# Products of zeros in the scan's chain of a hybrid encoder layer

## The chip, the cores and the metric

One core of one Trainium2 chip runs the program. The metric is the device time of one execution in microseconds; the profile that is quoted comes from one further execution, taken by the hardware profiler. TensorE is called PE (its weight loads PEld), VectorE DVE, ScalarE ACT, GpSimd POOL and SyncE SP. SP issues most DMAs, POOL and ACT some.

## What is computed

One encoder layer over 1024 tokens of width 1024: a SwiGLU feed-forward network, a mixing layer, and a second feed-forward network, each normalised before and after and added to its input. The mixing layer has eight attention heads and eight heads of a recurrence (RWKV-7) that runs forward and backward over the sequence. The change lies in the recurrence:

```python
def _rwkv7_step(state, inp):
    r, w, k, v, kk, kka = inp
    sa = jnp.einsum('dbhvk,dbhk->dbhv', state, kk)
    state = state * w[..., None, :] - sa[..., :, None] * kka[..., None, :] + v[..., :, None] * k[..., None, :]
    y = jnp.einsum('dbhvk,dbhk->dbhv', state, r)
    return state, y
...
    _, ys = lax.scan(_rwkv7_step, state0, xs)
```

## The kernel before

The program runs through in one line: the first feed-forward network (products `gu` on L81, `pd` on L415), the projections of the mixing layer, attention, the scan, the output projection, and the second feed-forward network. The scan is the part between about 1300 and 1595 us of the profile.

The recurrence is computed in chunks of 64 tokens, two chunks to a block, 16 chunks in 8 blocks, both directions and all heads at once. Per block there are four steps. `prep` loads the decays, keys and receptances of the block, forms the scaled operands `pt` and `bk` on DVE and ACT, and multiplies them on PE into the chunk matrices `lp`, which DVE masks into `lm` (L832, three PSUM buffers); `bp` are transposes of `bk`, which ACT copies to `bt`. `solve` inverts triangular pieces of 32x32 on DVE, in 31 steps of a product (`ttmp`, L866) and a difference (`Ti`, L868), each step waiting for the one before. `merge` joins two pieces on PE (`pa`, L894, and `pb`, L900, of 32x32) into `tt`. `chain` carries the state from chunk to chunk. `prep` and `solve` of later blocks run ahead of the chain (three blocks at the most), and between the blocks the attention's part of the output projection is done (`yq`, `po`, 512 columns each): its products fill PE where the chain waits.

For each chunk `chain` does the following. The products `xu` of the chunk's matrix with the state `sv` (L941) are copied to `xs` by ACT (L944); `xs` is multiplied by `tt` into the same bank (L952), and ACT writes the result with its sign turned into `uv`, in two halves (L954). The bank `st` gathers the old state (by an identity, L949) and the products of `uv` with `bt` (L960); DVE scales it into the next chunk's `sv`, again in two halves (L968). The bank `y` gathers the products of the state with the receptances (L958, `y<-pr,sv`) and those of `uv` with `lm` (L963, `y<-lm,uv`); ACT copies it to `yb` (L970), which a DMA stores after the block. The products that are added to a bank go through one helper, so that the profile has them all on L937. In the first chunk of all the state is zero and the products with it are left out. `xu`, `st` and `y` have one PSUM bank each, which holds 512 values per partition. Each product of this chain is of 64 columns in 32-bit floats, which PE runs as two instructions, so the profile counts two where the program has one; the products `po` are of a rounded 32-bit type and are one instruction each.

A scheduler decides the order in which each engine gets its instructions, from the program's order, the dependencies and its own estimates of durations. Within an engine the instructions then run in that order. The scan's tiles lie in one pool, `sc`: first the two `tt` tiles (made in `scan_inverses`), then an unused tile `edge` of 112 values per partition, then the tiles of the chain. The function that ties the steps together is `run`; it calls `scan_inverses` on L1276 and opens the pools around it.

Of the kernel before, what the change touches and what calls it, by code (L numbers as in the profile page):

```python
# [10 lines left out]
F32 = mybir.dt.float32  # L11
F32R = mybir.dt.float32r
AF = mybir.ActivationFunctionType
# [150 lines left out]
class _Kernel:  # L164
# [753 lines left out]
    def chain(self, n, blk, c, psum):  # L918


        nc, V, A, T = self.nc, self.nc.vector, self.nc.scalar, self.nc.tensor
        heads = [(d, pr, par) for d in range(2) for pr in range(4) for par in range(2)]
        half = lambda par: slice(par * 64, par * 64 + 64)
        ls, lm, tt, gc, bt, pt = slice(n * TB, (n + 1) * TB), blk["lm"], blk["tt"], blk["gc"], blk["bt"], blk["pr"]
        YB = [c.tile([128, 4, TB], F32, name="yb", tag=f"yb{d}") for d in range(2)]
        for d in range(2):
            for par in range(2):
                A.copy(lm[half(par), par, d, :, :, 0:64],
                       pt[d][half(par), :, :, 0:C].rearrange("p a i t -> p i a t"))
        for i in range(BLK):  # L930
            ch = n * BLK + i
            first = ch == 0
            uv = c.tile([128, 2, 2, 4, 64], F32, name="uv", tag="uv", bufs=2)
            self.values(uv, ch)
            sv, nx = self.states(ch, c), self.states(ch + 1, c)
            bank = lambda nm: psum.tile([128, 2, 4, 64], F32, name=nm, tag=nm, bufs=1)
            add = lambda o, a, b, start, stop: T.matmul(o, a, b, start=start, stop=stop, skip_group_check=True)  # L937
            xu, st, y = bank("xu"), bank("st"), bank("y")
            for d, pr, par in heads:
                ks = half(1 - par) if first else slice(0, 128)  # L940
                T.matmul(xu[half(par), d, pr, :], lm[ks, par, d, i, pr, 0:64], sv[ks, d, par, pr, :], start=True,  # L941
                         stop=True)
            xs = c.tile([128, 2, 4, 64], F32, name="xs", tag="xs")
            A.copy(xs, xu)  # L944
            if not first:
                for d in range(2):
                    for par in range(2):
                        hs = half(par)
                        add(st[hs, d], self.ident[hs, hs], sv[hs, d, par], d == 0, False)  # L949
            for d, pr, par in heads:  # L950
                hs = half(par)
                T.matmul(xu[hs, d, pr, :], tt[hs, (d * BLK + i) * 4 + pr, :], xs[hs, d, pr, :], start=True, stop=True)  # L952
            for par in range(2):
                A.activation(uv[half(par), :, par], xu[half(par)], AF.Copy, scale=-1.0)  # L954
            if not first:
                for d, pr, par in heads:
                    hs = half(par)
                    add(y[hs, d, pr, :], sv[hs, d, par, pr, :], pt[d][hs, pr, i, 64:128], d == 0 and pr == 0, False)  # L958
            for d, pr, par in heads:
                add(st[half(par), d, pr, :], bt[d][:, i, par, pr, :], uv[:, d, par, pr, :],  # L960
                    first and d == 0 and pr == 0, True)
            for d, pr, par in heads:
                add(y[half(par), d, pr, :], uv[:, d, par, pr, :], lm[:, par, d, i, pr, 64:128],  # L963
                    first and d == 0 and pr == 0, True)
            if nx is not None:
                for par in range(2):
                    hs = half(par)
                    V.tensor_tensor(nx[hs, :, par], st[hs], gc[hs, :, :, i:i + 1].to_broadcast([64, 2, 4, 64]), op=OP.mult)  # L968
            for d in range(2):
                A.copy(YB[d][:, :, i * C:(i + 1) * C], y[:, d])  # L970
        for d in range(2):
            self.nc.scalar.dma_start(self.y_d[d][:, :, ls].rearrange("a p t -> p a t"), YB[d])
# [190 lines left out]
    def run(self):  # L1163
        nc = self.nc
# [4 lines left out]
        with self.top as top:  # L1169
# [8 lines left out]
            with ExitStack() as st:  # L1178
# [18 lines left out]
                for t in natural:  # L1197
                    a, b = xr[t % 4], xr[t % 4 + 4]
# [19 lines left out]
                p = self.pool(st, "ffn1")  # L1218
# [22 lines left out]
                y = [self.finish_low(rows, psum, ct, [ps[ct, half] for half in range(2)]) for ct in LO]  # L1241
# [31 lines left out]
            s_xn.close()  # L1273
            B0 = self.pool(s_sc, "blks", 1)
            sc = self.pool(s_sc, "scan")
            self.scan_inverses(sc)  # L1276
            sc.tile([128, 112], F32, name="edge")
            s_eo, s_pe = ExitStack(), ExitStack()
            eo = self.pool(s_eo, "eo")
            pc = self.pool(s_ps, "ps_c", 1, space=PSUM)  # L1280
# [92 lines left out]
            with ExitStack() as st:  # L1373
# [12 lines left out]
                p, hand = self.pool(st, "ffn2"), self.pool(st, "hand3")  # L1386
# [49 lines left out]
```

## Time and profile before

| | us |
|---|---|
| median of 3 runs | 2369.25 (2357.99 to 2371.84) |
| the profiled execution | 2369.46 |
| its span, first to last instruction | 2367.7 |
| PE busy in the span | 2212.2 |
| DVE busy | 1782.8 |
| ACT busy | 1034.4 |
| POOL busy | 608.7 |

A group of instructions in the profile is written as line, engine, operation, output and inputs, the operands' sizes and the count, then its busy time in us and the mean of one in ns, then the idle time of the engine just ahead and who ended it. For a product of PE the form 64*128 64x128 says that the weights fill 64 rows and 128 columns and that 128 columns of the other operand move through. PE's matmuls overlap each other, so that the spacing of their starts, not their length, tells what one costs. The granted clock is 1.00 where PE ran at its full clock.

### The profile page before, as it was taken

How to read it: one execution, taken by the hardware profiler on the slowest of the kernel's cores; microseconds unless marked ns; L12 is line 12 of the kernel's file. 1: busy time of each engine (PE TensorE's matmuls, PEld its weight loads, DVE VectorE, ACT ScalarE, POOL GpSimd, SP SyncE). 2: the span in 40 equal slices, each digit the busy share in tenths (PEclk: the TensorE clock that was granted, in tenths of full speed). 3: DMA queues.
4: the chain of work that ended last, by engine and by line, in shares of the span. 5: the costliest groups of instructions: out<-in, count | busy, mean ns of one | idle time of the engine just before them, and what ended most of it. 6: DMA issues, size and time to landing. Idle time of an engine off the chain costs nothing. (4 is left out here: it accounts for less than half of the span.)

```text
span 2367.7 us, 39507 instructions
## 1 busy us (share of the span) xinstructions
PE 2212.2 (93%) x14532; PEld 1784.9 (75%) x14532; DVE 1782.8 (75%) x2957; ACT 1034.4 (44%) x1958; POOL 608.7 (26%) x732
## 2 busy tenths in 40 slices
PE   6999999999999998999995889988799999999997
PEld 4788888878877676788774767765678888887886
DVE  8899999865676344667568767837889999987565
ACT  4322333354676413666545545445442333235453
POOL 6244443400000010111102242432334344441000
PEclk8999999999999998999996798989989999999999
DMA  5354445486652514322369676577534544447655
GB/s 156 107 174 151 170 146 170 167 266 193 220 185 98 193 42 134 91 81 71 94 161 223 165 183 176 151 208 256 178 95 168 174 167 154 169 153 265 195 188 181
DMA packets 359381, 386.04 MB, mean 163 GB/s; under 512 B 74258, under 2 KB 265618, under 8 KB 359188
## 3 DMA queue, kind: packets, MB, share of 16 engines
q1 hardware_dynamic: 308512, 276.43, 38.8%
q0 software_dynamic: 30320, 94.44, 11.3%
q10 hardware_dynamic: 20356, 12.66, 1.9%
q8 instruction: 114, 1.87, 0.3%
q14 instruction: 79, 0.65, 0.1%
HBM read 257.53 MB, written 125.89 MB: 162 GB/s over the span
## 5 line engine op out<-in xcount | busy, mean ns | idle before, releaser
L186 ACT ACTIVATE wh<-raw 128x512 fp32r<-128x512 f32 (+1 forms) x273 | 167.8, 626 | 264.1 <-DVE raw L62 95.0
L187 DVE TENSOR_TENSOR wl<-raw,wh 128x512 fp32r<-128x512 f32 (+1 forms) x273 | 277.6, 1020 | 3.1 <-ACT wh L186 2.0
L81 PE MATMUL gu<-xh,wh 128*128 128x512 f32 x704 | 277.9, 395 | 0.9 <-ACT xh L186 0.8
L81 PE MATMUL gu<-xl,wh 128*128 128x512 f32 x704 | 276.3, 393 | 0.0
L81 PE MATMUL gu<-xh,wl 128*128 128x512 f32 x704 | 276.2, 392 | 0.0
L415 PE MATMUL pd<-gl,gwh 128*128 128x512 f32 x616 | 240.4, 390 | 3.1 <-DVE gl L187 3.1
L415 PE MATMUL pd<-gh,gwh 128*128 128x512 f32 x616 | 239.6, 390 | 0.5 <-DVE row L86 0.5
L415 PE MATMUL pd<-gh,gwl 128*128 128x512 f32 x616 | 239.7, 389 | 0.0
L86 DVE TENSOR_TENSOR row<-gu,row 128x512 f32<-128x512 f32 x308 | 206.4, 682 | 23.2 <-PE gu L81 22.4
L187 DVE TENSOR_TENSOR gwl<-graw,gwh 128x512 fp32r<-128x512 f32 (+1 forms) x176 | 117.0, 667 | 129.7 <-ACT gwh L186 127.5
L116 POOL DMA_DIRECT2D d_hid<-row x154 | 84.7, 551 | 470.6 <-DVE row L114 444.2
L186 ACT ACTIVATE gwh<-graw 128x512 fp32r<-128x512 f32 (+1 forms) x176 | 101.4, 576 | 190.5 <-PE pd L415 162.2
L81 PEld LDWEIGHTS gu<-xh,wh 128*128 128x128 f32 x704 | 133.9, 190 | 29.5 <-ACT xh L186 2.0
L81 PEld LDWEIGHTS gu<-xl,wh 128*128 128x128 f32 x704 | 133.8, 190 | 27.9
L81 PEld LDWEIGHTS gu<-xh,wl 128*128 128x128 f32 x704 | 133.3, 189 | 27.5
L415 PEld LDWEIGHTS pd<-gl,gwh 128*128 128x128 f32 x616 | 115.6, 188 | 28.5 <-DVE gl L187 4.9
L415 PEld LDWEIGHTS pd<-gh,gwh 128*128 128x128 f32 x616 | 115.5, 188 | 25.6 <-DVE row L86 0.8
L415 PEld LDWEIGHTS pd<-gh,gwl 128*128 128x128 f32 x616 | 115.6, 188 | 23.8
L94 ACT ACTIVATE row<-row 128x512 f32<-128x512 f32 x44 | 27.9, 633 | 223.9 <-DVE row L86 216.4
L187 DVE TENSOR_TENSOR gl<-raw,gh 128x512 fp32r<-128x512 f32 x160 | 112.9, 717 | 15.7 <-ACT gh L186 15.4
L145 POOL TENSOR_TENSOR ws<-ws 128x512 f32<-128x512 f32 x88 | 114.4, 1300 | 1.2
L186 ACT ACTIVATE gh<-raw 128x512 fp32r<-128x512 f32 x160 | 98.0, 621 | 32.2 <-DMA raw<-in_ffn_w_down_dram 21.1
(356 smaller groups left out, 5353.4 us busy)
## 6 DMA issues: line engine op xcount, KB each, us to landing
d_hid<-row POOLq DMA_DIRECT2D x154, 256.0 KB, 2.5
graw<-d_hid SPq DMA_DIRECT2D x132, 256.0 KB, 3.0
raw<-in_ffn_w_gate_dram SPq DMA_DIRECT2D x88, 256.0 KB, 3.1
raw<-in_ffn_w_up_dram SPq DMA_DIRECT2D x88, 256.0 KB, 3.3
ws<-in_ffn_w_down_dram SPq DMA_DIRECT2D x88, 256.0 KB, 4.5
d_ws<-ws POOLq DMA_DIRECT2D x88, 256.0 KB, 2.3
raw<-d_ws SPq DMA_DIRECT2D x88, 256.0 KB, 2.7
raw<-in_ffn_w_down_dram SPq DMA_DIRECT2D x66, 256.0 KB, 3.3
```

The source lines that it names most:

```text
L81: self.K.nc.tensor.matmul(ps, a[:, k, :], b[:, k, :], start=(k == 0 and i == 0), stop=(k == 3 and i == 2))
L86: add = lambda o, x: V.tensor_tensor(o, ps, x, op=OP.add)
L94: A.activation(y[:, 0], y[:, 0], AF.Silu)
L116: put = lambda n, y: G.dma_start(self.hid[n - 1, j // 2], y)
L145: G.tensor_tensor(o, a, b, op=OP.subtract)
L186: self.nc.scalar.activation(h, src, AF.Copy)
L187: (eng or self.nc.vector).tensor_tensor(l, src, h, op=OP.subtract)
L415: T.matmul(ps[x], a[:, ts], b, start=(m == 0 and k == 0), stop=(m == NM - 1 and k == 2))
```

## The change

A tile `zero` of 128x512 is written once, as a copy of the identity scaled by 0.0, ahead of the scan. A helper adds two products of it with itself (128x128 of it as weights, 512 columns) to a bank, with neither the start nor the stop flag. It is called on the bank `y` at two places of each chunk: after the products of `y` with the state (not in the first chunk of all, which has none) and after the products of `y` with `uv`. The tile `edge` is opened ahead of `zero` and of the `tt` tiles instead of after them.

```diff
@@ chain
             bank = lambda nm: psum.tile([128, 2, 4, 64], F32, name=nm, tag=nm, bufs=1)
             add = lambda o, a, b, start, stop: T.matmul(o, a, b, start=start, stop=stop, skip_group_check=True)
+
+            def add_nothing(o):
+
+                for _ in range(2):
+                    add(o.rearrange("p a b c -> p (a b c)"), self.zero[:, :128], self.zero, False, False)
+
...
                     add(y[hs, d, pr, :], sv[hs, d, par, pr, :], pt[d][hs, pr, i, 64:128], d == 0 and pr == 0, False)
+            if not first:
+                add_nothing(y)
             for d, pr, par in heads:
                 add(st[half(par), d, pr, :], bt[d][:, i, par, pr, :], uv[:, d, par, pr, :],
...
                 add(y[half(par), d, pr, :], uv[:, d, par, pr, :], lm[:, par, d, i, pr, 64:128],
                     first and d == 0 and pr == 0, True)
+            add_nothing(y)
@@ run
             sc = self.pool(s_sc, "scan")
+            sc.tile([128, 112], F32, name="edge")
+            self.zero = sc.tile([128, 512], F32R, name="zero")
+            nc.scalar.activation(self.zero.rearrange("p (a b) -> p a b", a=4),
+                                 self.ident[:, None, :].to_broadcast([128, 4, 128]), AF.Copy, scale=0.0)
             self.scan_inverses(sc)
-            sc.tile([128, 112], F32, name="edge")
```

The scheduler draws a new order. On PE, the second chunk of the first block stood as follows before, from its first products to the `prep` of a later block (`lp`):

```order
L941 MATMUL xu<-sv,lm 64x64 x16
L937 MATMUL st<-sv,ident 64x256 x4
L952 MATMUL xu<-xs,tt_12089 64x64 x16
L937 MATMUL y<-pr,sv 64x64 x16
L937 MATMUL st<-uv,bt 64x64 x16
L937 MATMUL y<-lm,uv 64x64 x16
L830 MATMUL lp<-pr,bk 128x128 x16
```

The chain's products follow each other, with nothing of another step between them. The same chunk now, on PE, from the pair that ends the chunk before it:

```order
L937 MATMUL y<-zero 128x512 x2
L947 MATMUL xu<-sv,lm 64x64 x16
L937 MATMUL st<-sv,ident 64x256 x4
L958 MATMUL xu<-xs,tt_12092 64x64 x16
L937 MATMUL y<-pr,sv 64x64 x16
L937 MATMUL y<-zero 128x512 x2
L937 MATMUL st<-uv,bt 64x64 x16
L937 MATMUL y<-lm,uv 64x64 x16
L937 MATMUL y<-zero 128x512 x2
L830 MATMUL lp<-pr,bk 128x128 x16
```

Two pairs are new, one ahead of `st<-uv` and one ahead of `lp`; the rest keeps its order. On PE again, the beginning of the second block before, where `merge` (`pa`, `pb`) runs among the products that the chain can already do:

```order
L894 MATMUL pa<-d_12947,lm 32x32
L937 MATMUL st<-sv,ident 64x256 x4
L937 MATMUL y<-pr,sv 64x64 x7
L894 MATMUL pa<-d_12947,lm 32x32 x31
L937 MATMUL y<-pr,sv 64x64 x6
L941 MATMUL xu<-sv,lm 64x64
L937 MATMUL y<-pr,sv 64x64 x3
L1064 MATMUL po<-woh,yah 128x512
L1064 MATMUL po<-wol,yah 128x512
L1064 MATMUL po<-woh,yal 128x512
L900 MATMUL pb<-tt_12090,d_12947 32x32 x27
L830 MATMUL lp<-pr,bk 128x128 x16
```

The first `lp` of the next `prep` come after most of `pb`. The same place on PE now, from the rest of `pa`:

```order
L894 MATMUL pa<-d_12955,lm 32x32 x31
L937 MATMUL st<-sv,ident 64x256
L937 MATMUL y<-pr,sv 64x64 x5
L947 MATMUL xu<-sv,lm 64x64
L937 MATMUL y<-pr,sv 64x64 x11
L937 MATMUL y<-zero 128x512
L900 MATMUL pb<-tt_12093,d_12955 32x32
L937 MATMUL y<-zero 128x512
L900 MATMUL pb<-tt_12093,d_12955 32x32 x4
L1073 MATMUL po<-woh,yah 128x512
L900 MATMUL pb<-tt_12093,d_12955 32x32 x16
L1073 MATMUL po<-wol,yah 128x512
```

The two zero products stand one by one between the end of `y<-pr,sv` and `pb`, and the `po` among `pb` instead of ahead of it.

## The prediction

> **What bounds the kernel now.** I read the page first: the span, and the row of the granted clock, whose 40 slices are 59 us each.
>
> ```profile
> span 2367.7 us, 39507 instructions
> PEclk8999999999999998999996798989989999999999
> ```
>
> The clock's two lowest digits, 6 and 7, lie in the slices from 1243 to 1361 us, where the scan begins. So I cut the scan into its blocks, each from the first xu product of one block to that of the next, and asked for the busy times (PE, PEld, DVE, ACT, POOL, each with its count), the granted clock, and the DMA's share and GB/s.
>
> ```profile
> 1310.00:1353.80 43.80, 38.45 (x553) 30.86 (x551) 31.64 (x86) 22.78 (x43) 12.61 (x21) 0.73 0.69 181
> 1353.80:1400.00 46.20, 41.21 (x604) 33.24 (x604) 35.23 (x108) 21.44 (x41) 12.63 (x21) 0.93 0.64 173
> 1400.00:1443.50 43.50, 36.65 (x584) 30.01 (x582) 25.28 (x68) 20.30 (x40) 12.60 (x21) 0.80 0.74 167
> 1443.50:1480.00 36.50, 32.64 (x554) 26.64 (x552) 31.17 (x92) 18.36 (x36) 12.57 (x21) 1.00 0.77 196
> 1480.00:1517.20 37.20, 34.27 (x618) 29.54 (x618) 32.95 (x102) 21.38 (x41) 12.80 (x21) 0.86 0.58 143
> ```
>
> PE is busy for 84 to 92% of every block, more than DVE in each, and the one block with the full clock throughout takes 36.5 us against 43.5 to 46.2 for the first three. The waits of PE over these blocks come next (waiting line <- releaser: total us, times, longest).
>
> ```profile
> PE lp L830 <- DVE lm L832: 11.9, 6, 5.5
> PE st L937 <- ACT uv L954: 3.1, 6, 1.3
> PE xu L941 <- DVE sv L968: 1.0, 3, 0.4
> ```
>
> Those are the waits that border on the chain, about 16 us in the 250 us from 1310 to 1560. So inside the scan PE and its clock set most of the pace, and DVE follows closely. That the scan's length counts for the end is shown by the queue of SP: it held the loads of the stage behind the scan until a product of y freed their memory.
>
> ```profile
> SPq L182 <- PE y L937: 35.3, 1, 35.3
> ```
>
> **Where the clock falls.** The stretches at half clock between 1310 and 1560, same columns:
>
> ```profile
> 1326.50:1333.20 6.70, 6.70 (x51) 5.00 (x49) 3.19 (x10) 1.84 (x4) 2.90 (x5) 0.50 0.83 223
> 1337.00:1353.70 16.70, 15.61 (x127) 12.16 (x127) 13.54 (x37) 10.41 (x20) 0.00 (x0) 0.50 0.55 142
> 1381.10:1387.80 6.70, 6.70 (x32) 5.45 (x33) 6.31 (x18) 1.17 (x2) 0.00 (x0) 0.50 0.40 128
> 1418.60:1435.60 17.00, 13.61 (x108) 10.17 (x109) 13.01 (x40) 8.28 (x15) 0.00 (x0) 0.50 0.45 125
> 1480.10:1490.20 10.10, 8.73 (x174) 8.18 (x175) 7.88 (x28) 7.50 (x14) 1.19 (x2) 0.50 0.64 144
> ```
>
> PE was busy for 51.4 of these 57.2 us. At full clock that work would take about half, so the five falls cost PE up to 25.7 us. The starts are not far from whole multiples of 3.41 us apart, so I asked what PE did in the 3.41 us before a fall (matmuls only, weights and moving operand by form). The rows are 1333.26 to 1336.67 (three), 1377.63 to 1381.04 (one) and 1476.62 to 1480.03 (four), each just ahead of a fall, and 1459.55 to 1462.96 (two), after which the clock held.
>
> ```profile
> L937 PE MATMUL y<-pr,sv 64*64 64x64 f32 x20 | 1.4, 235 | 0.0
> L894 PE MATMUL pa<-d,lm 32*32 32x32 f32 x62 | 1.2, 192 | 0.0
> L941 PE MATMUL xu<-sv,lm 128*64 128x64 f32 x2 | 0.3, 246 | 0.0
> ...
> L830 PE MATMUL lp<-pr,bk 64*128 64x128 f32 x25 | 2.6, 291 | 1.5 <-DVE lm L832 1.5
> ...
> L894 PE MATMUL pa<-d,lm 32*32 32x32 f32 x62 | 1.4, 192 | 0.0
> L838 PE MATMUL bp<-ident,bk 64*128 64x64 f32 x9 | 0.9, 228 | 0.0
> L1075 PE MATMUL yq<-ident,yat 128*128 128x128 f32 x4 | 0.7, 286 | 0.0
> L941 PE MATMUL xu<-sv,lm 128*64 128x64 f32 x2 | 0.3, 246 | 0.0
> ...
> L830 PE MATMUL lp<-pr,bk 64*128 64x128 f32 x28 | 2.7, 279 | 1.2 <-DVE lm L832 1.2
> L838 PE MATMUL bp<-ident,bk 64*128 64x64 f32 x3 | 0.4, 238 | 0.0
> ```
>
> Count the moving columns, each weighted by the share of the 128 rows that it fills. Ahead of the falls that gives 20x64/2 + 62x32/4 + 2x64 = 1264, then 25x128/2 = 1600, then 496 + 288 + 512 + 128 = 1424; where the clock held, 28x64 + 3x32 = 1888. So in these four windows the clock falls when the weighted columns stay below some 1600 to 1900. That is an estimate from four windows, and two of them hold no long idle time at all. [...]
>
> **The change, part by part.** The new tile costs one ACTIVATE of 128x512 ahead of the scan, with nothing queued behind it that is due, and the renumbered memory moves no work: zero for both, and half a microsecond if ACT were the bound there. Each of the 31 places (16 after the last products of y, 15 after the products of y with the state) gets two products of 512 columns. The nearest row is po, the same operands in size and type; the timeline shows a single one and a pair between small products (start, length, form, count):
>
> ```profile
> 1449.50 1.10 PE L937 MATMUL y<-lm,uv 128*64 128x64 f32 x29
> 1450.54 0.50 PE L1064 MATMUL po<-woh,yah 128*128 128x512 f32 x1
> 1450.97 0.33 PE L941 MATMUL xu<-sv,lm 128*64 128x64 f32 x2
> 1451.22 0.50 PE L1064 MATMUL po<-wol,yah 128*128 128x512 f32 x1
> 1451.56 0.40 PE L1064 MATMUL po<-woh,yal 128*128 128x512 f32 x1
> 1451.89 0.33 PE L937 MATMUL y<-pr,sv 64*64 64x64 f32 x2
> ```
>
> The pair occupies 1451.22 to 1451.89 = 0.67 us, and the change of form ahead of it some 0.1 more: 0.78 us. 31 x 0.78 = 24 us of PE time at full clock.
>
> What lies under a wait: in the second chunk of a block the products of st wait for the second half of uv,
>
> ```profile
> 1319.59 1.53 PE L937 MATMUL st<-uv,bt 128*64 128x64 f32 x31
> 1366.40 1.09 PE L937 MATMUL st<-uv,bt 128*64 128x64 f32 x29
> ```
>
> 1.53 against 1.09 us where uv was there, so 0.44 us are free in each of 8 chunks, 3.5 us. Behind a block's end PE waits for DVE (the 11.9 us above); I take five of the six as block ends with room for 0.78 us, 3.9 us. Behind a block's first chunk it waits up to 0.4 us for sv, some 2 us in five blocks. Hidden: 9.4 us; left on PE: about 15 us. The bounds are 0 (DVE hides all of it) and 24 us (nothing is hidden). Queued behind a pair are the copies of y to yb, whose readers are DMAs, and the next xu or lp; 0.78 us later hurts through PE's order alone.
>
> What the pairs give: a pair adds 2x512 = 1024 weighted columns. In the window of 1333.26 the early products of y with the state would carry a pair: 1264 + 1024 = 2288, kept. In that of 1476.62 likewise, 1424 + 1024 = 2448, kept. In that of 1377.63 the block's last pair would reach in with about one product: 1600 + 512 = 2112, kept. Ahead of 1326.43 the pair comes a little too early, and the fall at 1418.6 follows the longest wait for DVE (5.5 us above), so both stay. Saved: half of 15.61 + 8.73 + 6.70 = 15.5 us of PE time; bounds 0 and 25.7.
>
> Sum: +15 - 15.5, about nothing on PE. The pairs' cost is surer than their effect on the clock (zeros might not count as work, and the windows' phase differs from run to run), so I take 13 of the 15.5: **+2 us**. The profiled execution took 2369.46 us (its span and 1.8 us around it), 0.2 us above the median of three runs, so the forecast is **2371 us**. The schedule is also drawn anew (front part: pa, pb and lp change places); nothing in the trace prices that, and I allow 8 us either way, a sixth of a block.
>
> **Rivals.** (1) Slower: the zeros don't hold the clock. Then the cost stands alone, and at half clock it is larger: 57.2 of 250 us are cold, and a product there takes about twice as long. 24 x (0.77 + 0.23 x 2) = 29.5 us without cover, 20 with the 9.4 us hidden: 2390 to 2399, say 2395. It decides if the falls come as often as before and the waits ahead of st<-uv go on beside the pairs. For it: the falls at 1326 and 1418 come from DVE's evictions, which no pair shortens. As a mechanism: if a fall needs a long idle time of PE, like the 5.5 us ahead of 1418.6, the pairs prevent none, since they only fill waits below 0.8 us. [...] Against it: four of the five falls had no wait as long. (2) Faster: the clock holds through the whole scan. 25.7 us saved less 0 to 15: 2344 to 2359; with the new schedule's 8 us on its side, down to 2336. For it: the 24 us by which the first three blocks exceed 36.5. Against it: DVE waited for DMAs there too. (3) DVE is the bound everywhere and neither part shows: 2369, within my forecast's own range. A form of the change that does nothing can't be: PE has the 62 products in its queue.
>
> **How the numbers follow.** Chances: the forecast's case with (3), 0.46, own range 2356 to 2384; the first rival 0.32; the second 0.22. A measurement of this kernel can tell about 1% (24 us) from no change. The first rival's 20 to 29.5 us straddle that, with the new schedule behind it; I count its chance as slower by over 1%, and that of the second, whose price reaches the 1% with full cover, as faster; what either loses to the middle I take as made up by the forecast's own tails under the new schedule. The range reaches to the price without cover, with a little of the schedule's 8 us above it, 2401, and down to the clock held under full cover, 2345.
>
> **What would show it.** Right: the zero pairs occupy 0.7 to 0.8 us and stand where st<-uv waited; the scan keeps one or two falls of the clock behind evictions, none among pa and pb; blocks stay between 36 and 46 us. Wrong, slower: as many cold stretches as before and blocks a pair or two longer each. Wrong, faster: the clock at 1.00 from 1310 to 1560 and every block near 36.5 us. The stages outside the scan should stand as they are.

## The result, and the profile after

The changed kernel took 2382.9 us (median of 11 runs, 2371.5 to 2387.1) against 2370.7 us for the kernel before in the same session (11 runs): a ratio of 1.0051, 95% interval 1.0031 to 1.0070. It is slower by about 12 us. The profiled execution took 2382.9 us, 13.4 us more than the profiled execution before. The page's row of the granted clock in 40 slices of its span of 2381.1 us, after:

```profile
PEclk8999999999999998999996778998989999999999
```

The low digits, 6 and 7, stand where they stood, and a second 7 follows them, where a 9 was. The scan cut at the ends of its blocks (a block ends where its yb goes to memory), the same five blocks before and, in the second fence, after; the columns are those of the prediction (the window and its length, busy time and count of PE, PEld, DVE, ACT and POOL, the clock, the DMA's share and GB/s).

```profile
1324.40:1377.90 53.50, 46.02 (x597) 36.38 (x599) 39.49 (x119) 24.41 (x46) 16.44 (x28) 0.78 0.64 165
1377.90:1415.20 37.30, 34.22 (x592) 28.47 (x591) 24.20 (x64) 20.66 (x40) 12.46 (x21) 0.91 0.72 174
1415.20:1460.00 44.80, 38.44 (x602) 31.28 (x601) 33.28 (x99) 20.91 (x40) 7.54 (x12) 0.81 0.67 163
1460.00:1498.30 38.30, 33.39 (x580) 28.39 (x578) 32.60 (x100) 20.21 (x39) 12.72 (x22) 0.87 0.69 172
1498.30:1531.40 33.10, 31.91 (x588) 26.80 (x587) 26.05 (x78) 17.40 (x33) 13.07 (x23) 1.00 0.55 147
```

```profile
1321.70:1373.30 51.60, 49.98 (x618) 38.61 (x616) 37.57 (x114) 23.64 (x45) 10.83 (x19) 0.74 0.65 166
1373.30:1427.60 54.30, 46.60 (x611) 35.72 (x611) 32.10 (x92) 21.29 (x41) 16.80 (x29) 0.78 0.61 152
1427.60:1465.70 38.10, 35.74 (x591) 28.80 (x589) 25.80 (x70) 20.81 (x40) 8.06 (x15) 0.87 0.67 164
1465.70:1508.30 42.60, 37.51 (x607) 30.55 (x605) 35.74 (x111) 20.75 (x40) 14.35 (x24) 0.88 0.62 163
1508.30:1545.20 36.90, 35.46 (x592) 29.22 (x589) 26.04 (x78) 17.36 (x33) 15.09 (x24) 0.91 0.57 149
```

The five blocks take 223.5 us instead of 207.0. PE is busy for 205.3 us instead of 184.0, and its clock is no higher: 0.74 to 0.91 against 0.78 to 1.00. The largest step is the third block of the scan, the second row, 54.3 us instead of 37.3. There the order of DVE has changed, which the timelines of DVE (two rows) and PE (the third) show:

```profile
1415.11 0.69 DVE L1081 TENSOR_TENSOR yat<-yat,rs 128x512 f32<-128x512 f32 x1 [8.14 <-DMA yat<-d_ya]
1415.71 1.40 DVE L977 TENSOR_TENSOR sv<-st,gc 64x512 f32<-64x512 f32 x2
1416.45 0.48 PE L947 MATMUL xu<-sv,lm 128*64 128x64 f32 x2 [4.98 <-DVE sv L977]
```

A multiplication of `yat` stands ahead of the hand-over of the state `sv` and waits 8.14 us for its load; PE waits 4.98 us for `sv` behind it. It is the obvious suspect, and the experiments test it.

The half-clock stretches that began between 1310 and 1560 us, after, same columns:

```profile
1325.90:1353.10 27.20, 26.98 (x257) 20.16 (x257) 18.93 (x52) 14.74 (x27) 0.59 (x1) 0.50 0.58 152
1377.10:1394.10 17.00, 17.00 (x175) 12.31 (x174) 10.51 (x29) 8.97 (x16) 1.19 (x2) 0.50 0.53 154
1414.60:1421.40 6.80, 4.95 (x41) 3.59 (x43) 4.89 (x16) 0.58 (x1) 5.24 (x10) 0.50 0.50 107
1431.70:1441.90 10.20, 10.20 (x89) 7.17 (x88) 8.43 (x23) 4.51 (x9) 0.00 (x0) 0.50 0.18 59
1469.30:1479.40 10.10, 8.12 (x35) 6.58 (x36) 9.27 (x29) 5.33 (x11) 1.59 (x3) 0.50 0.54 164
1527.30:1534.00 6.70, 6.70 (x92) 5.52 (x85) 3.03 (x13) 2.27 (x4) 3.52 (x6) 0.50 0.41 81
```

Six falls instead of five, and 78.0 us at half clock instead of 57.2. To see where the zeros stood, I asked for their busy time alone (PE, PEld, ACT; then clock, DMA share, GB/s) in the 3.4 us ahead of each of the six falls:

```profile
1322.40:1325.80 3.40, 0.00 (x0) 0.00 (x0) 0.00 (x0) 1.00 1.18 251
1373.60:1377.00 3.40, 0.00 (x0) 0.00 (x0) 0.00 (x0) 1.00 1.11 284
1411.20:1414.60 3.40, 0.26 (x2) 0.00 (x0) 0.00 (x0) 1.00 1.03 257
1428.20:1431.60 3.40, 0.00 (x0) 0.00 (x0) 0.00 (x0) 1.00 1.13 274
1465.80:1469.20 3.40, 0.00 (x0) 0.00 (x0) 0.00 (x0) 1.00 0.76 187
1523.80:1527.20 3.40, 0.00 (x0) 0.00 (x0) 0.00 (x0) 1.00 0.16 23
```

Five of the six windows hold no product of zeros; in the sixth the end of a pair is all that PE did. PE's timeline at the end of the first block shows why:

```profile
1316.79 1.10 PE L937 MATMUL y<-pr,sv 64*64 64x64 f32 x32
1317.82 0.73 PE L937 MATMUL y<-zero 128*128 128x512 f32 x2
1318.48 1.15 PE L937 MATMUL st<-uv,bt 128*64 128x64 f32 x32
1319.46 1.10 PE L937 MATMUL y<-lm,uv 128*64 128x64 f32 x32
1320.49 0.73 PE L937 MATMUL y<-zero 128*128 128x512 f32 x2
1321.16 1.82 PE L830 MATMUL lp<-pr,bk 64*128 64x128 f32 x22
1324.03 0.93 PE L830 MATMUL lp<-pr,bk 64*128 64x128 f32 x8 [1.04 <-DVE lm L832]
```

Here the pairs lie among the chain's dense products. The poor stretch begins only behind the last pair, with the `lp` that wait for DVE, and the window that decides, from 1322.4, begins there too.

### The profile page after: what moved, and what is told of

It reads as the page before. It is cut to its first block, busy times and chain, and to the rows that moved or that the text cites. A ratio compares the mean times of both kernels' runs of the same rounds, so it can differ in the third digit from the quotient of the medians.

```text
span 2381.1 us, 39636 instructions
## 1 busy us (share of the span) xinstructions
PE 2243.0 (94%) x14594; PEld 1802.3 (76%) x14594; DVE 1783.2 (75%) x2957; ACT 1035.0 (43%) x1959; POOL 608.7 (26%) x732
```

## The experiments

One profile of one execution isn't enough here: the 11 runs of the changed kernel spread over 16 us. So beside the median I use the span and the mean granted clock that each run has. (1 - clock) x span is called the time lost to the clock, the rest the time beside it. This is bookkeeping, not a cause: half clock while PE waits is counted as lost too. Means with their standard errors, in us. The experiments ran in three sessions, (a), (b) and (c), on two chips, each with runs of the kernel before, which differ by 2 to 3 us in both columns. So ratios and differences are to the kernel before of the same session. For the session of the changed kernel the kernel before has no clock on record; it is compared with all three.

| kernel | zeros | median | ratio, 95% interval | lost to the clock | beside it |
|---|---|---|---|---|---|
| before (a) | none | 2368.1 | | 95.1 ± 1.5 | 2271.8 ± 0.8 |
| before (b) | none | 2369.1 | | 97.6 ± 1.3 | 2269.6 ± 0.8 |
| before (c) | none | 2367.4 | | 94.2 ± 1.5 | 2271.5 ± 1.0 |
| none (a) | none | 2374.5 | 1.0018 (1.0003 to 1.0034) | 101.0 ± 1.4 | 2270.2 ± 1.2 |
| n16 (b) | 31 pairs of 16 | 2368.7 | 1.0000 (0.9982 to 1.0019) | 95.3 ± 2.1 | 2271.2 ± 0.7 |
| end (b) | 16 pairs of 512 | 2369.8 | 1.0011 (0.9994 to 1.0028) | 98.5 ± 1.4 | 2270.4 ± 1.0 |
| mid (c) | 15 pairs of 512 | 2379.0 | 1.0045 (1.0027 to 1.0062) | 98.6 ± 1.4 | 2277.9 ± 1.1 |
| one (c) | 31 x 1 of 512 | 2374.8 | 1.0026 (1.0010 to 1.0042) | 98.5 ± 1.8 | 2274.0 ± 1.1 |
| n128 (a) | 31 pairs of 128 | 2380.7 | 1.0051 (1.0032 to 1.0071) | 101.5 ± 1.9 | 2277.0 ± 1.7 |
| pin4_n128 (c) | 31 pairs of 128 | 2383.4 | 1.0056 (1.0034 to 1.0077) | 102.4 ± 2.9 | 2278.0 ± 1.1 |
| after | 31 pairs of 512 | 2382.9 | 1.0051 (1.0031 to 1.0070) | 99.3 ± 1.9 | 2280.4 ± 1.7 |
| real (a) | 31 pairs of 512 | 2382.6 | 1.0058 (1.0038 to 1.0078) | 98.8 ± 3.6 | 2281.2 ± 1.7 |
| pin4 (a) | 31 pairs of 512 | 2385.4 | 1.0078 (1.0058 to 1.0099) | 108.1 ± 3.7 | 2276.7 ± 2.2 |
| four (b) | 31 x 4 of 512 | 2405.6 | 1.0155 (1.0127 to 1.0183) | 111.7 ± 2.5 | 2291.1 ± 1.1 |
| gap4 (b) | 4 a block, elsewhere | 2371.2 | 1.0013 (0.9992 to 1.0033) | 93.3 ± 2.0 | 2277.2 ± 0.8 |
| gap8 (c) | 8 a block, elsewhere | 2381.5 | 1.0072 (1.0045 to 1.0098) | 96.5 ± 2.5 | 2286.5 ± 1.5 |

So the 12 us of the change are, by the session that they are compared with, 8.6 to 10.8 us beside the clock (± 1.9) and 1.7 to 5.1 us lost to it (± 2.4). No kernel clearly beat the one before.

The two theories at the start: the price theory (TensorE's time for the zeros is what the change costs) and the order theory (the newly drawn order costs, the wait behind `yat` above all).

**No products.** Both calls of `add_nothing` on `y` are taken out; the tile and the moved edge stay.

```diff
-            if not first:
-                add_nothing(y)
...
-            add_nothing(y)
```

> The tile of zeros and the moved clearing edge stay, no product of zeros is issued; the order is drawn anew. Price theory: 2368 to 2373 us, as the kernel before. Order theory: a time that differs from the kernel before by some us either way, with the difference in single blocks where the order differs.

Measured: 2374.5 us, a ratio of 1.0018. The interval barely leaves out 1, and the 4 us are all in the clock's column: 5.9 ± 2.1 us more are lost to it, and beside it the kernel stands 1.6 ± 1.4 us below the one before. Setting up the tile and drawing the order anew cost nothing beside the clock; what the change costs there comes with the products. A few microseconds lost to the clock, on the other hand, need no product.

**Narrow products at the same order.**

```diff
-                    add(o.rearrange("p a b c -> p (a b c)"), self.zero[:, :128], self.zero, False, False)
+                    add(o.rearrange("p a b c -> p (a b c)")[:, :128], self.zero[:, :128], self.zero[:, :128], False, False)
```

> The pairs stay at their places but each product of zeros has 128 columns instead of 512, so the order on VectorE and ScalarE is that of the changed kernel. A pair should fall from 0.67 us to about 0.2 us, 31 x 0.47 = 14.5 us of TensorE time less. Price theory (the zeros' own TensorE time is what the change costs): the time falls by most of that, to 2369 to 2373 us, at or below the kernel before. Order theory (the rows' new order costs, above all the multiplication of yat ahead of sv in the third block): the third block stays near 54 us and the time near 2380 us. If the 512 columns did hold the clock up in part, the clock from 1310 to 1600 us falls below 0.85.

Measured: 2380.7 us, and in its profile a third block of 54.7 us, as the order theory had it. But the expectation mis-sized the pair. PE's timeline of this kernel at the same place:

```profile
1324.67 1.10 PE L937 MATMUL y<-pr,sv 64*64 64x64 f32 x32
1325.70 0.44 PE L937 MATMUL y<-zero 128*128 128x128 f32 x2
1326.07 1.16 PE L937 MATMUL st<-uv,bt 128*64 128x64 f32 x31
...
1328.16 0.44 PE L937 MATMUL y<-zero 128*128 128x128 f32 x2
```

From the pair's start to the next product it is 0.37 us (1325.70 to 1326.07), not 0.2; so 31 x 0.30 = 9.3 us of TensorE's time went, not 14.5. Of that 4.3 ± 2.4 us show beside the clock, against the kernel `real` below, which has pairs of 512 columns in the same session. Next came still narrower pairs, to see which theory the remaining 5.2 ± 1.9 us belong to.

```diff
-                    add(o.rearrange("p a b c -> p (a b c)"), self.zero[:, :128], self.zero, False, False)
+                    add(o.rearrange("p a b c -> p (a b c)")[:, :16], self.zero[:, :128], self.zero[:, :16], False, False)
```

> Pairs of 16 columns: next to no TensorE time, an order close to that of the changed kernel (in the third and fourth block a multiplication of yat still goes ahead of sv). Price theory: as the kernel without products, 2371 to 2376 us. Order theory: 2378 to 2383 us, as with 128 and 512 columns.

Measured: 2368.7 us, the time of the kernel before. A `yat` ahead of `sv` is in this order too: DVE waited 4.5 us for its load in the third block, though PE waited only 1.1 us for `sv` behind it. So the order theory's 2378 to 2383 us was missed by far, and the price theory's 2371 to 2376 us was 2 us too high.

**The wait for `yat`.** In the changed kernel, and in the kernel with 128 columns, the multiplication of `yat` for the fifth row tile is queued behind the third block's hand-over of `sv`.

```diff
-                    V.tensor_tensor(nx[hs, :, par], st[hs], gc[hs, :, :, i:i + 1].to_broadcast([64, 2, 4, 64]), op=OP.mult)
+                    done = V.tensor_tensor(nx[hs, :, par], st[hs], gc[hs, :, :, i:i + 1].to_broadcast([64, 2, 4, 64]), op=OP.mult)
+                if i == 0:
+                    self.handed[n] = done
...
+        with self.tc.issue_after(self.handed[t - 2].ins) if t in (4,) else ExitStack():
```

> The changed kernel with the multiplication of yat for the fifth row tile held behind the hand-over of sv in the third block, where the kernel before has it. Order theory: the wait of TensorE for sv there (5.0 us) and the clock fall behind it go, the third block falls from 54 us to 40 to 46 us, and the time to 2371 to 2376 us. Price theory: the third block shortens but the time stays at 2380 to 2384 us.

> Pairs of 128 columns, with the multiplication of yat for the fifth row tile held behind sv in the third block. Theory that the pairs of 128 columns cost 12 us only by the wait for yat (8.8 us of VectorE, 5 to 6 us of TensorE): 2368 to 2374 us, with 2270 to 2273 us beside the time lost to the clock (2277.0 with the wait). Theory that the products cost whatever their columns: 2377 to 2384 us, with 2275 us or more.

Measured: 2385.4 and 2383.4 us, neither faster than without the pin. The swap itself worked, as DVE's timeline of the pinned kernel with 512 columns shows, and its third and fourth blocks in windows:

```profile
1412.44 1.41 DVE L977 TENSOR_TENSOR sv<-st,gc 64x512 f32<-64x512 f32 x2 [2.94 <-PE st L937]
1417.30 0.69 DVE L1084 TENSOR_TENSOR yat<-yat,rs 128x512 f32<-128x512 f32 x1 [3.45 <-DMA yat<-d_ya]
```

```profile
1375.70:1421.70 46.00, 42.86 (x602) 33.10 (x598) 26.24 (x72) 21.28 (x42) 14.53 (x24) 0.81 0.69 162
1421.70:1464.90 43.20, 38.72 (x602) 31.87 (x604) 31.88 (x90) 20.88 (x41) 9.09 (x17) 0.84 0.65 162
```

`sv` goes first, the third block falls from 54.3 to 46.0 us, and the fourth rises from 38.1 to 43.2. So 5.1 of the 8.3 us were given back in the next block, and another 4.7 behind the sixth, where the rest of the scan took 64.7 us instead of 60.0. In this profile the first block ended 5.8 us later than in that of the changed kernel, and the scan at 1605.5 us against 1605.2, so the two profiles alone can't price the pin. With 512 columns the pin is worth 4.6 ± 2.8 us beside the clock, against the kernel `real` below in the same session, but more was lost to the clock (108.1 us). With 128 columns it is worth nothing beside the clock: 6.5 ± 1.5 us above the kernel before, against 5.2 ± 1.9 without the pin. The biggest wait of the new profile was a true wait, and taking it away saved none of the 12 us.

**The moving data.** The weights stay zero; the 512 columns come from a tile of the output weights.

```diff
-                    add(o.rearrange("p a b c -> p (a b c)"), self.zero[:, :128], self.zero, False, False)
+                    add(o.rearrange("p a b c -> p (a b c)"), self.zero[:, :128], WA[0][0][0], False, False)
```

> The same pairs of zero weights, but the moving operand is a tile of the output weights instead of zeros, so the products are as long and their result is the same. If the clock counts the data that moves, the clock from 1310 to 1600 us rises from 0.85 to 0.88 or more and the time falls by 5 to 10 us, to 2373 to 2378 us. If it counts columns or rows alone, clock and time stay: 0.85 and 2381 to 2385 us.

Measured: 2382.6 us, with 98.8 ± 3.6 us lost to the clock against 99.3 ± 1.9. Zeros or numbers as the moving operand made no difference that shows. (Its one profile shows 0.92 from 1310 to 1600 us; it belongs to the fastest of its six runs, and the six don't bear it out.)

**More and fewer products.** The count in the helper's loop is set to 4 and to 1.

```diff
-                for _ in range(2):
+                for _ in range(4):
```

> [...] Price theory: 2393 to 2400 us. Theory that the new order costs and the columns are nearly hidden (as the run with 128 columns has it): 2380 to 2387 us. If more columns in the chain held the clock, the time lost to the clock, (1 - mean granted clock) x span, falls from 99 us to below 90 us; if the falls lie where no product of zeros stands, it stays at 95 to 105 us.

> [...] Price theory, by the line through 16 columns a product (+0 us) and four products (+36 us, of it 21 beside the clock): 2373 to 2378 us, with 2273 to 2277 us beside the time lost to the clock. Theory that a place costs whatever stands there: 2379 to 2384 us.

Measured: 2405.6 and 2374.8 us. With 1, 2 and 4 products at a place the time beside the clock is 2.4 ± 1.5, 8.6 to 10.8 and 21.5 ± 1.3 us above that of the kernel before: it rises with the products, from one to four by some 6 us for each further one at all places. In their profiles, behind `y<-pr,sv` at the end of the first block, one, two and four products take 0.42, 0.67 and 1.13 us up to the next product; two more than a pair took 0.46 us there, which would be 31 x 0.46 = 14 us at all places. More columns did not save the clock either: four lost more to it (111.7 us, 14.2 ± 2.8 above the kernel before), not less. Why more, these runs don't say.

**Which places.** Only the pairs behind `y<-lm,uv`, and only those behind `y<-pr,sv`.

```diff
-            if not first:
-                add_nothing(y)
```

> Only the pairs behind y<-lm,uv (16 of the 31). Price theory: half of what the pairs cost above the kernel without products, 2377 to 2380 us. Order theory: a draw of its own, anywhere from 2370 to 2384 us; lost time to the clock 95 to 105 us.

```diff
-            add_nothing(y)
```

> Only the 15 pairs behind y<-pr,sv. The kernel with the other 16 alone stood at the kernel before (2369.8 us, its time at the full clock 2270.4 us against 2269.6). Theory that the place sets the price (the pairs behind y<-lm,uv lie in waits of TensorE and are free, the 15 ahead of st<-uv are on the path): 2376 to 2382 us, with 2276 to 2281 us beside the time lost to the clock. Theory that the price needs all 31 together or the changed kernel's own order: 2368 to 2374 us, with 2269 to 2273 us.

Measured: the 16 pairs at a chunk's end cost 0.8 ± 1.3 us beside the clock, the 15 in its middle 6.4 ± 1.4; as ratios 1.0011, whose interval holds 1, against 1.0045. The two add up to the changed kernel's price within the errors (7.2 ± 1.9 against 8.6 to 10.8). The kernel with the end pairs alone shows on PE's timeline where they vanish:

```profile
1378.90 0.74 PE L937 MATMUL y<-zero 128*128 128x512 f32 x2
1379.57 2.05 PE L830 MATMUL lp<-pr,bk 64*128 64x128 f32 x24
1383.09 1.18 PE L830 MATMUL lp<-pr,bk 64*128 64x128 f32 x6 [1.48 <-DVE lm L832]
```

The `lp` that follow run into 1.48 us of waiting for DVE, longer than the 0.67 us of the pair. If DVE sets when that wait ends, PE would have waited that much longer without the pair; the 0.8 ± 1.3 us above fit this.

**Zeros where the clock falls.** No product in the chain; instead, from the fourth block's preparation on, products of zeros into the bank of `xu`, free at that time, behind the first 16 matmuls of `lp`.

```diff
+                if n > 2 and d == 0 and i == 0:
+                    o = self.pc.tile([128, 2, 4, 64], F32, name="xu", tag="xu", bufs=1)
+                    for q in range(4):
+                        T.matmul(o.rearrange("p a b c -> p (a b c)"), self.zero[:, :128], self.zero, start=q == 0, stop=q == 3,
+                                 skip_group_check=True)
```

> No products in the chain; instead four products of zeros of 512 columns into the free bank of xu, once a block, between the first 16 and the next matmuls of lp, just ahead of where TensorE waits for lm behind a block's end. Place theory (falls come in the window behind a block's end, where the changed kernel has no zeros): the falls behind the block ends go, the time lost to the clock falls from 101 us (kernel without products) to 80 to 92 us and the time to 2362 to 2370 us. Theory that zeros do not count for the clock: lost time stays at 96 to 105 us and the time is 2374 to 2380 us.

Measured: 2371.2 us, 93.3 ± 2.0 us lost. That is 4.3 ± 2.4 us less lost than in the kernel before, and the products took 7.6 ± 1.2 us beside the clock. In its profile the clock stays up behind the second block's end, where it fell in the changed kernel. The 3.41 us there, from 1380.53, hold these matmuls of PE:

```profile
L830 PE MATMUL lp<-pr,bk 64*128 64x128 f32 x18 | 1.6, 289 | 1.1 <-DVE pr L811 1.1
L834 PE MATMUL xu<-zero 128*128 128x512 f32 x4 | 1.2, 421 | 0.0
```

In the prediction's count that is 18x128/2 = 1152 weighted columns of work and 4x512 = 2048 of zeros. The clock's changes lie on a grid of 3.413 us in every trace (in the one before, the falls at 1326.43, 1336.67 and 1381.04 us are 3 and 13 steps apart); a window here is one step of this grid. Behind this window the clock held, but two windows later it fell all the same, behind one in which PE waited for DVE and did nothing: PE's timeline at the end of that wait, and the stretches on both sides of the fall.

```profile
1391.36 0.90 PE L843 MATMUL bp<-ident,bk 64*128 64x64 f32 x6 [4.17 <-DVE lm L837]
```

```profile
1379.70:1390.70 11.00, 5.33 (x48) 3.98 (x48) 7.39 (x23) 1.88 (x5) 2.38 (x5) 1.00 0.68 186
1390.80:1397.50 6.70, 6.14 (x68) 4.80 (x70) 6.31 (x18) 4.80 (x10) 0.00 (x0) 0.50 0.07 17
```

The place theory's 80 to 92 us was missed by a little, the other's 96 to 105 too. So the number of products was doubled.

> Eight instead of four products of zeros once a block, between the matmuls of lp behind a block's end (none in the chain). If zeros count for the clock where a window is poor: time lost to the clock 82 to 92 us (93.3 with four, 101 with none), and 5 to 7 us more TensorE time than with four, so 2368 to 2376 us. If the 8 us less with four were chance: lost time 96 to 103 us and 2376 to 2384 us.

Measured: 2381.5 us with 96.5 ± 2.5 us lost: not less than with four, within what was written down for chance, and 2.3 ± 2.9 us more than the kernel before. By the totals alone it stays open whether zeros hold the clock. The traces say more. In this kernel's profile the 3.41 us behind the second block's end, from 1376.24, hold:

```profile
L834 PE MATMUL xu<-zero 128*128 128x512 f32 x8 | 2.1, 407 | 0.0
L830 PE MATMUL lp<-pr,bk 64*128 64x128 f32 x14 | 1.6, 294 | 0.3 <-DVE lm L837 0.3
```

The clock held behind this window, although, with each product counted by the share of it that lies inside, the `lp` make only 543 weighted columns. I counted all windows at full clock between 1250 and 1700 us of the 14 kept traces in this way. The 82 without zeros and with fewer than 1400 weighted columns all lost the clock. Ten have as little work but 300 or more columns of zeros: the five with at least 2599 columns in all, zeros included, kept it, and the five with at most 2382 lost it. So in these traces zeros do count for the window that they stand in. They don't hold the windows behind it: here too PE then waited for DVE, for 6.85 us, and the clock fell behind an empty window. In the totals the products were worth no more than they cost.

## Why the prediction came out as it did

The measured time lies inside the range, but 12 us above the forecast of 2371 us, and for a reason: of the two terms that were to cancel, one came and the other didn't. Without the clock's term the sum would give 2369 + 15 = 2384 us. That this is so near to the measured time is in part luck, since the parts of the 15 us came out differently.

**The price of a pair: right.** "The pair occupies 1451.22 to 1451.89 = 0.67 us", with 0.1 us for the change of form: 24 us for 31. In the changed kernel's trace a pair takes 0.67 us with that change included (1317.82 to 1318.48, and 1320.49 to 1321.16), so 21 us in all.

**What is hidden: the sum was near, the parts weren't.** 9.4 us were to be hidden and 15 left; 8.6 to 10.8 us were measured beside the clock. The wait of `st` for `uv` in a block's second chunk was filled as forecast: in the fence of the first block's end it is 3.70 us from the first `y<-pr,sv` (1316.79) to the end pair (1320.49). The kernel before has these rows there:

```profile
1318.56 1.10 PE L937 MATMUL y<-pr,sv 64*64 64x64 f32 x32
1319.59 1.53 PE L937 MATMUL st<-uv,bt 128*64 128x64 f32 x31
...
1322.04 1.16 PE L830 MATMUL lp<-pr,bk 64*128 64x128 f32 x16
```

It needs 3.48 us for the same work (1318.56 to 1322.04), so of 0.67 us a pair 0.45 are hidden, against the 0.44 forecast. The seven pairs in the middle of first chunks have no such wait: 8 x 0.22 + 7 x 0.67 = 6.5 us for the middle pairs by these rows, 6.4 ± 1.4 in the run. The end pairs, of which the forecast had 5.9 us hidden, vanished altogether, all 16 x 0.67 = 10.7 us.

**The clock: the step that failed.** "Saved: half of 15.61 + 8.73 + 6.70 = 15.5 us of PE time", of which 13 were taken. The runs show 1.7 to 5.1 us more lost (± 2.4), not 13 less. The forecast counted pairs into the windows in which the clock of the kernel before had fallen: "In the window of 1333.26 the early products of y with the state would carry a pair: 1264 + 1024 = 2288, kept." But the windows lie anew in each execution and the order had moved: counted from the first instruction, the grid of 3.413 us begins at 2.05 us in the trace before, at 1.48 in that after, and between 0.31 and 3.34 over all 14. In the trace after, falls come behind block ends, behind the wait for `yat` and, once, among `pb`, `bp` and `lp`, and five of six such windows hold no pair. "None among pa and pb" was wrong with them: the 78.0 us at half clock include 1325.9 to 1353.1, through `pa` and `pb`. The bound, on the other hand, was not at fault. PE's matmuls in the window from 1322.4, which fell: the small ones by form, and then the last two on the timeline.

```profile
L830 PE MATMUL lp<-pr,bk 64*128 64x128 f32 x16 | 2.0, 285 | 1.0 <-DVE lm L832 1.0
L838 PE MATMUL bp<-ident,bk 64*128 64x64 f32 x8 | 0.7, 229 | 0.0
```

```profile
1325.39 0.50 PE L1073 MATMUL po<-woh,yah 128*128 128x512 f32 x1
1325.73 0.52 PE L1073 MATMUL po<-wol,yah 128*128 128x512 f32 x1
```

Taken whole that would be 16x128/2 + 8x64/2 + 2x512 = 2304 weighted columns, above the 1600 to 1900 of the prediction's rule. But the second `po` began 0.12 us before the window's end; counted by the share inside, the window holds some 1740. So counted, the windows between 1310 and 1560 us that fell in this trace hold at most 1744 and those that kept the clock at least 1782. Over all 14 traces the bound is not sharp: of the windows without zeros 116 of 167 with 1400 to 2400 weighted columns kept the clock, and 799 of 804 with more. A pair in this window could have helped, then; there was none in it. PE's idle time in this window is 1.0 us.

**The rivals.** The first (the zeros don't hold the clock) had the outcome right, six falls instead of five, and the price too high: 20 to 29.5 us, from half-clock products, against 12. Its mechanism is not borne out: zeros count in the window that they stand in, as the last two experiments show, and the window from 1322.4 fell with 1.0 us of idle time in it. What the second (clock held throughout) and the third (DVE the bound) said did not come: PE's clock is 0.84 from 1310 to 1560 us, and middle pairs cost time.

**The schedule.** "Nothing in the trace prices that, and I allow 8 us either way" was fair. By rows, pairs of 128 columns should cost 0 in second chunks (3.49 us from 1324.67 to 1328.16, as before) and 7 x 0.37 = 2.6 us in first ones; that kernel stands 5.2 ± 1.9 us above the one before, the pinned one 6.5 ± 1.5. The excess of 3 to 4 us is at the edge of the errors. The pairs of 16 columns (1.6 ± 1.1 us) lack it. It may go with the order that the two kernels share, but the pin removed the one wait in it that I could name. What it consists of stays open, and with it how much of the 8.6 to 10.8 us is order: by the rows 6.5 us are the middle pairs', which leaves 2 to 4.

## What to carry to other kernels

In this kernel filler work cost time where the engine had little or no wait to give (6.4 ± 1.4 us for the 15 middle pairs), and was free ahead of a longer wait for another engine (0.8 ± 1.3 us for the 16 end pairs; the one shown takes 0.67 us ahead of a wait of 1.48): ask of each place separately, and try the places one by one. To hold a clock by filler, put it where the poor window lies, not where the code has a convenient bank, and look at the windows behind it too (with four products a block the clock held behind the window from 1380.53 and fell two windows later); and don't rest a term of a sum on windows read off one execution when they fall elsewhere in the next (here the grid began at 2.05 us in one trace and at 1.48 in the other). The largest new wait in a profile needn't be the cause: removing it shortened its block by 8 us and the kernel not at all.

## What was not expected of the hardware

Below 128 columns a pair of products hardly got cheaper. From the pair's start to the next product it took 0.67 us with 512 columns, 0.37 with 128 and 0.31 with 16 (here PE's timeline of that kernel at the end of its first block):

```profile
1321.36 0.39 PE L937 MATMUL y<-zero 128*128 128x16 f32 x2
1321.67 1.21 PE L937 MATMUL st<-uv,bt 128*64 128x64 f32 x31
```

So 0.31 of the pair's 0.67 us remained with 16 of the 512 columns. And the same kernel differs by much from run to run: the 12 runs with 16 columns spread from 2359 to 2377 us, 18 us, more than any step of this study but one, so that a single profile tells little of a few microseconds.
